# Normalising the heads' outputs inside the transposing product, and other pieces for the last token tile

## The chip, the cores and the metric

One Trainium2 chip, one core. The metric is the device time of one launch in microseconds; of several runs the median is given. A profile is one execution recorded by the hardware; its times are counted from the first instruction.

## What is computed

One layer of a hybrid backbone for 512 latent tokens and 128 context tokens (640 rows), width 1024, float32. From the reference, cut to what the change touches:

```
z = h @ w_in                                     # q, k, v, g_ret, x_lru, g_lru, m_ret, m_lru
o = o_f + o_b                                    # retention, 4 heads, 512 columns per head
o = o * rsqrt(mean(o * o, -1) + EPS)             # per token and head
o = o.reshape(B, L, D_RET_V) * gn_w * silu(g_ret)
ret_out = o @ w_ret_down
merged = sigmoid(m_ret) * ret_out + sigmoid(m_lru) * lru_out
out = x + gate * (merged @ w_out)
y = rmsnorm(out, final_norm_w)                   # y_sample (512 tokens), y_prompt (128 tokens)
```

The two recurrent (RG-LRU) directions and the cached states are computed beside it.

## The kernel before

Tokens are handled as five tiles of 128 (four of the latents, one of the prompt) or, transposed, as 640 columns. Products are made of split operands: a matrix is kept as a rounded part (float32r) and a rest, and `mm3` (L413) issues three products for one. Stage A makes most columns of z in transposed form and stores them to DRAM. Then come four heads; then the product with `w_ret_down` (the loop over `DOWN`, 128 output columns at a time, each in two halves of k), the product with `w_lru_down`, and `w_out` with the end.

For head h: `v_product` (four steps of 7.5 us of TensorE work each), `inter`, `scores`, `kv_state`, `attend`. `attend` adds up `o[t]` for the five token tiles (128 tokens by 512 columns, tokens on the partitions), with the squares' sums in `ssq`. The job `norm` (L1477) takes the root and the reciprocal into `rst` and multiplies each `o[t]` by its column on VectorE (L1486). Later, `y_unit(h, i)` (L1518) for i = 0 to 3 transposes the 128-column block i of the five `o[t]` into two PSUM banks `z` and `zp_` (L1522), with `ident` as the moving operand; a job multiplies that by the gate tile `sg` (L1532 for 512 columns, L1535 for 128) and stores it to DRAM, from where `y_job` loads it again as `yf` and splits it into `yh` and `yl` for the `DOWN` loop. The four units of heads 0 to 2 stand inside the next head's `v_product`; those of head 3 stand ahead of steps 1 and 2 of the `DOWN` loop, two and two. So there are 16 units of 5 transposes.

Order: TensorE's instructions come in the order of the code. ACT's and VectorE's come from a planner (`Plan`, L93), which keeps planned clocks for the engines, gives every operation a planned cost (`Vh(n)` is 0.55 n + 150 ns on VectorE, a unit is 560 ns on TensorE) and picks among the jobs that are ready by priority. Each engine then executes its own list in order. All DMAs are issued by SP, in the order in which they were written out.

Tiles: wide tiles (128x640) come from `W6`, with 11 places in the heads' stage. q and k of a head, split, take 8 of them from their loading until `scores` is over; gate tiles `sg` take one each until stored. `sg0` and `sg1` are loaded after `attend`, `sg2` after unit 0's job and `sg3` after unit 1's. A place given back with a store outstanding is planned as free 4 us later; the load that takes it waits for the store. Weights arrive in 512 KB pieces in 4 raw buffers and are split into 3 slab pairs. There are 8 PSUM banks.

The end: `w_out` is used token tile by token tile. Each tile is made in pieces of output columns (L1848): two of 512 for tiles 0 to 3; for tile 4, the prompt's, 512, 256 and 256. A piece is 24 products (8 k, three each), and then `finish_part` (L1790): product with the gate (L1800), add of the input (L1802), on ACT the squares' sum (L1804), product with the norm weight (L1806); a small sum (`finish_sum`, L1816 and L1818 in tile 4); and after the last piece `finish_end` (L1820): root on ACT, reciprocal (L1826), ACT scales the second 512 columns (L1832), VectorE the first (L1835), and SP issues a store of each (L1836), the second half's first. A job of a piece follows the job of the piece before it.

Of the kernel before, what the change touches and what calls it, by code (L numbers as in the profile page):

```python
# [12 lines left out]
MUL, ADD, SUB = ALU.mult, ALU.add, ALU.subtract  # L13
# [79 lines left out]
class Plan:  # L93
# [14 lines left out]
    def job(self, gen, name=None, prio=2.0):  # L108
        self.seq += 1
        j = Job(gen, prio, self.seq, self.time() + self.LAG)  # L110
        self.jobs.append(j)
        if name:
            self.named[name] = j
        self.advance(j)
        return j
# [64 lines left out]
    def need(self, name):  # L180
        j = self.named.get(name)
        assert j is not None, f"nothing makes {name}"
        self.finish(j, name)
# [77 lines left out]
def A(n, table=None):  # L261
    return ("act", 0.85 * n + 190.0, table)


def V(n):
    return ("dve", 1.042 * n + 150.0)


def Vh(n):
    return ("dve", 0.55 * n + 150.0)  # L270


def If(f):
    return ("if", f)
# [28 lines left out]
def tile_hybrid_step(  # L303
# [14 lines left out]
    nc = tc.nc  # L318
    S = Plan()
    act, dve, pool, pe = nc.scalar, nc.vector, nc.gpsimd, nc.tensor  # L320
# [13 lines left out]
    W6, WL = Slots(S), Slots(S)  # L334
# [5 lines left out]
    def wide(name, r=False):  # L340
        return W6.take([128, NT], F32R if r else F32, name)
# [45 lines left out]
    ident = cst.tile([128, 128], F32, name="ident")  # L387
# [15 lines left out]
    rst = cst.tile([128, 8], F32, name="rst")  # L403
# [9 lines left out]
    def mm3(out, lh, ll, rh, rl, start, stop, **kw):  # L413
        pe.matmul(out=out, lhsT=lh, rhs=rh, start=start, stop=False, **kw)  # L414
        pe.matmul(out=out, lhsT=lh, rhs=rl, start=False, stop=False, **kw)  # L415
        pe.matmul(out=out, lhsT=ll, rhs=rh, start=False, stop=stop, **kw)  # L416
        S.pe += 3 * (out.shape[-1] / 2.4 + 13.4)
# [4 lines left out]
    def bank():  # L422
        if not banks.items:
            S.until(lambda: banks.items)
        t = banks.take([128, 512], F32, "z")
        w = t_when.pop(id(t))
        if w > S.pe and S.cur is None:
            S.lost.append((S.pe, w - S.pe, "bank"))
            S.pe = w
        return t  # L430
# [167 lines left out]
    def store(key, t, w=NT):  # L598
        if key not in kept:
            kept[key] = scr.tile([128, w], F32, name="_".join(str(a) for a in key))  # L600
        nc.sync.dma_start(out=kept[key], in_=t[:, 0:w])
        stored[key] = arrives(128 * w * 4)
# [406 lines left out]
    def after(name):  # L1009
        return If(lambda: S.over(name))  # L1010
# [250 lines left out]
    def narrow(name, r=False):  # L1261
        return W5.take([128, 512], F32R if r else F32, name)
# [23 lines left out]
    def strip_job(h):  # L1286
        ds, s = d["ds"], d["strip"]
        yield Vh(896)
        dve.tensor_scalar(s, ds, sp[:, 24 + h:25 + h], None, op0=MUL)
        yield V(896)  # L1290
        dve.scalar_tensor_tensor(s, ds, lg[:, h:h + 1], s, op0=MUL, op1=ALU.min)
        yield A(896, "exp")
        act.activation(s, s, AF.Exp)

    qk, v, o, pt, kd = {}, {}, {}, {}, {}
# [166 lines left out]
    def attend(h):  # L1462
        def ev(t, ps):
            if t == 4:
                yield If(W5.room())
                o[t] = narrow("o")
                yield A(512)
                act.activation(o[t], ps, AF.Copy)
            else:
                yield after(f"i{h}{t}1")  # L1470
                yield V(512)
                dve.tensor_tensor(o[t], o[t], ps, op=ADD)
            yield A(512)
            act.activation(ps, o[t], AF.Square, accum_out=ssq[:, t:t + 1])
            banks.give(ps)

        def norm():  # L1477
            for t in range(5):
                yield after(f"o{h}{t}")
            yield A(5, "sqrt")  # L1480
            act.activation(rst[:, 0:5], ssq[:, 0:5], AF.Sqrt, scale=1.0 / DV, bias=epsc)
            yield V(5)
            dve.reciprocal(rst[:, 0:5], rst[:, 0:5])
            for t in range(5):
                yield Vh(512)
                dve.tensor_scalar(o[t], o[t], rst[:, t:t + 1], None, op0=MUL)  # L1486

        need(f"st{h}4")
        ps = bank()
        mm3(ps, pt[4][0], pt[4][1], v[4][0], v[4][1], True, True)  # L1490
        job(ev(4, ps), f"o{h}4", prio=1.0)
        for t in range(4):
            ps = bank()
            c = slice(128 * t, 128 * t + 128)
            for j in range(4):
                need(f"st{h}{j}")
                need(f"v{h}{j}")
                mm3(ps, pt[j][0][:, c], pt[j][1][:, c], v[j][0], v[j][1], j == 0, j == 3)
                S.pump()
            job(ev(t, ps), f"o{h}{t}", prio=1.0)  # L1500
        for i in range(5):
            for x in (pt[i] if i < 4 else ()) + v[i]:
                W5.give(x)
        job(norm(), f"y{h}", prio=1.0)
        job(strip_job(h + 1), f"strip{h + 1}", prio=3.0) if h + 1 < NH else None
        for i in range(4):
            job(sg_job(h, i), f"sg{h}{i}", prio=5.0)

    sg = {}

    def sg_job(h, i):
        if i > 1:
            yield after(f"yT{h}{i - 2}")
        yield If(is_kept(("g", h, i)))
        yield If(W6.room())
        sg[i] = fetch(("g", h, i), "sg")

    def y_unit(h, i):  # L1518
        need(f"y{h}")
        z, zp_ = bank(), bank()  # L1520
        for t in range(5):
            pe.transpose(z[:, 128 * t:128 * t + 128] if t < 4 else zp_[:, 0:128], o[t][:, 128 * i:128 * i + 128], ident)  # L1522
        S.pe += 560.0
        if i == 3:
            for t in range(5):
                W5.give(o.pop(t))

        def ev():
            yield after(f"sg{h}{i}")
            s = sg[i]  # L1530
            yield V(512)
            dve.tensor_tensor(s[:, 0:512], s[:, 0:512], z, op=MUL)  # L1532
            banks.give(z)
            yield V(128)
            dve.tensor_tensor(s[:, 512:640], s[:, 512:640], zp_[:, 0:128], op=MUL)  # L1535
            banks.give(zp_)
            store(("y", h, i), s)
            W6.give(s, 4000.0)

        job(ev(), f"yT{h}{i}", prio=1.2)  # L1540
        S.pump()
# [42 lines left out]
    for h in range(NH):  # L1584
        for kk in v_first if h == 0 else v_product(h):
            if h and kk:
                y_unit(h - 1, kk - 1)
            hook(h, f"v{kk}")
        if h:
            y_unit(h - 1, 3)  # L1590
        if h == NH - 1:
            hTp.__exit__(None, None, None)
            ytp, yr = open_pool("ytp", "right")
            yr.tile([128, 56], F32, name="edge")
            W6y.add(yr, [f"y{i}" for i in range(16)])
            for i in range(8):
                job(y_job(i // 4, i % 4, W6y), f"y_{i}", prio=3.0)
        inter(h)
        scores(h)
        if h + 1 < NH:  # L1600
            fetch_qk(h + 1)
        hook(h, "sc")
        kv_state(h)
        hook(h, "kv")
        attend(h)
        hook(h, "at")
# [116 lines left out]
    for m in range(8):  # L1723
        zs = [bank(), bank()]
        for k in range(NB):
            b = NB * m + k
# [29 lines left out]
        if m == 0:  # L1756
            b = bank()
# [62 lines left out]
    def finish_end(t, n):  # L1820
        q = fsq[:, 3 * t + n - 1:3 * t + n]
        pre = fsq[:, 15 + t:16 + t]
        yield A(1, "sqrt")
        act.activation(q, q, AF.Sqrt, scale=1.0 / D, bias=pre)
        yield Vh(1)
        dve.reciprocal(q, q)  # L1826
        dst = y_sample[128 * t:128 * t + 128, :] if t < 4 else y_prompt
        for b in (1, 0):
            u = fin_u[t, b][:, 0:512]
            if b:  # L1830
                yield A(512)
                act.activation(u, u, AF.Copy, scale=q)  # L1832
            else:
                yield Vh(512)
                dve.tensor_scalar(u, u, q, None, op0=MUL)  # L1835
            nc.sync.dma_start(out=dst[:, 512 * b:512 * b + 512], in_=u)  # L1836
            W6.give(fin_u[t, b], 4000.0)
            W6.give(xr[t, b])

# [6 lines left out]
    load_xr(0)  # L1846
    wo = {}
    parts = [(t, 512 * b, 512, b) for t in range(4) for b in range(2)]  # L1848
    parts += [(4, 0, 512, 0), (4, 512, 256, 1), (4, 768, 256, 2)]

    def finish(t, a, c0, n, i):
        end = 2 if t == 4 else 1
        if i:
            yield after(f"f{t}{i - 1}")
        yield from finish_part(t, a[:, 0:n], c0, n, i)
        banks.give(a)
        if i == end - 1:
            yield from finish_sum(t, end + 1)
        if i == end:
            yield from finish_end(t, end + 1)  # L1860
# [131 lines left out]
```

## Time and profile before

| | us |
|---|---|
| three runs, median (lowest to highest) | 999.16 (998.46 to 999.55) |
| profiled execution, its time | 999.01 |
| its span (first to last instruction) | 997.2 |
| TensorE matmul busy (PE) | 981.6 |
| TensorE weight load busy (PEld) | 918.0 |
| VectorE busy (DVE) | 732.3 |
| ScalarE busy (ACT) | 543.6 |
| GpSimd busy (POOL) | 2.2 |

PE and PEld are two views of TensorE: weight loads lie beside products, and products are pipelined, so the duration of one product (its latency) is longer than the distance from its start to the next one's. An idle time of an engine is listed with what ended it. The chain of work that ended last is followed back from the last instruction, at each step to what released it. The granted clock is TensorE's, as a share of 2.4 GHz; the profiled execution's mean is 0.997.

### The profile page before, as it was taken

Reading aid. Unit: us, or ns where it says so; the run is one execution under the profiler, and the core shown is the slowest. Engines: PE = TensorE matmul, PEld = TensorE weight load, DVE = VectorE, ACT = ScalarE, POOL = GpSimd, SP = SyncE. Lnnn points to the kernel's source line nnn. Section 1 sums busy time; section 2 is a strip of 40 time slices with the busy share of each in tenths; the row PEclk is TensorE's granted clock in tenths of the full one; section 3 lists DMA queues with packets and bytes.
Section 4 is the critical chain, followed back from the end, with each engine's and each line's share of the span. In section 5 each row is a group of like instructions: output and inputs, shape, how many; then the busy total and the mean of one; then the engine's idle time right before and its main releaser. Section 6 shows DMA issues by size and latency. Waiting matters only on the chain.

```text
span 997.2 us, 15542 instructions
## 1 busy us (share of the span) xinstructions
PE 981.6 (98%) x6079; PEld 918.0 (92%) x6079; DVE 732.3 (73%) x1133; ACT 543.6 (55%) x856; POOL 2.2 (0%) x13
## 2 busy tenths in 40 slices
PE   9999999999999999999999999999899999999997
PEld 8889999999999999999888888888789999999886
DVE  4699977779986799783775887877768877646554
ACT  6665554486544765652468596485574535324222
POOL 0000000000000000000000000000000000000000
PEclk9999999999999999999999999999999999999999
DMA  9745444333553335344532635454627554745312
GB/s 328 247 138 171 156 142 138 127 126 131 182 172 128 111 130 178 134 138 164 190 116 101 203 116 176 136 175 153 206 93 290 191 184 165 240 124 176 118 64 84
DMA packets 62167, 158.15 MB, mean 159 GB/s; under 512 B 6906, under 2 KB 10126, under 8 KB 62094
## 3 DMA queue, kind: packets, MB, share of 16 engines
q1 hardware_dynamic: 62094, 157.16, 46.9%
q8 instruction: 47, 0.77, 0.3%
q14 instruction: 26, 0.21, 0.1%
HBM read 119.51 MB, written 37.63 MB: 158 GB/s over the span
## 4 chain that ended last, share of the span: by engine, by line
PE 91%; DVE 4%; ACT 3%; issue 1%; DMA 1%; POOL 0%; DVEq 0%; POOLq 0%; ACTq 0%
PE z L414 29%; PE z L415 29%; PE z L416 29%; PE b L736 1%; PE z L1522 1%; ACT hf L294 1%; DVE sl L420 1%; ACT hTh L294 1%; DVE hTl L294 1%; DMA y<-sg 0%; DMA yf<-y 0%; ACT sh L539 0%; PE z L781 0%; ACT gt L1181 0%; DVE st L1416 0%
## 5 line engine op out<-in xcount | busy, mean ns | idle before, releaser
L420 DVE TENSOR_TENSOR sl<-raw,sh 128x1024 fp32r<-128x1024 f32 (+1 forms) x128 | 133.2, 1045 | 50.2 <-ACT sh L505 49.8
L505 ACT ACTIVATE sh<-raw 128x1024 fp32r<-128x1024 f32 (+1 forms) x96 | 96.8, 1013 | 120.2 <-PE z L415 75.9
L414 PE MATMUL z<-sh,sh 128*128 128x320 f32 x512 | 158.5, 310 | 0.7 <-ACT p L1007 0.7
L416 PE MATMUL z<-sh,sl 128*128 128x320 f32 x512 | 158.4, 309 | 0.0
L415 PE MATMUL z<-sl,sh 128*128 128x320 f32 x512 | 158.4, 309 | 0.0
L414 PE MATMUL z<-hTh,sh 128*128 128x320 f32 x432 | 134.6, 311 | 1.1 <-ACT hTh L294 1.1
L415 PE MATMUL z<-hTl,sh 128*128 128x320 f32 x432 | 133.4, 309 | 0.7 <-DVE hTl L294 0.7
L416 PE MATMUL z<-hTh,sl 128*128 128x320 f32 x432 | 133.2, 308 | 0.0
L414 PEld LDWEIGHTS z<-sh,sh 128*128 128x128 f32 x512 | 96.1, 188 | 1.3 <-ACT p L1007 1.3
L415 PEld LDWEIGHTS z<-sl,sh 128*128 128x128 f32 x512 | 96.1, 188 | 0.0
L416 PEld LDWEIGHTS z<-sh,sl 128*128 128x128 f32 x512 | 96.1, 188 | 0.0
L414 PEld LDWEIGHTS z<-hTh,sh 128*128 128x128 f32 x432 | 81.1, 188 | 3.9 <-issue 2.5
L415 PEld LDWEIGHTS z<-hTl,sh 128*128 128x128 f32 x432 | 81.1, 188 | 1.1 <-DVE hTl L294 1.1
L416 PEld LDWEIGHTS z<-hTh,sl 128*128 128x128 f32 x432 | 81.1, 188 | 0.0
L414 PE MATMUL z<-yh,sh 128*128 128x320 f32 x256 | 79.4, 310 | 1.6 <-ACT gt L1181 1.5
L415 PE MATMUL z<-yl,sh 128*128 128x320 f32 x256 | 79.2, 309 | 1.0 <-DVE yl L420 1.0
L416 PE MATMUL z<-yh,sl 128*128 128x320 f32 x256 | 79.0, 309 | 0.0
L414 PE MATMUL z<-sh,hTh 128*128 128x512 f32 x160 | 63.7, 398 | 0.0
L415 PE MATMUL z<-sl,hTh 128*128 128x512 f32 x160 | 63.2, 395 | 0.0
L416 PE MATMUL z<-sh,hTl 128*128 128x512 f32 x160 | 63.2, 395 | 0.0
L1054 ACT ACTIVATE p<-z 128x320 f32<-128x320 f32 x32 | 14.0, 437 | 67.3 <-PE z L416 67.3
L414 PEld LDWEIGHTS z<-yh,sh 128*128 128x128 f32 x256 | 48.1, 188 | 2.2 <-ACT gt L1181 1.7
(256 smaller groups left out, 2240.3 us busy)
## 6 DMA issues: line engine op xcount, KB each, us to landing
raw<-in_w_str_dram SPq DMA_DIRECT2D x131, 512.0 KB, 3.8
adr<-in_w_ada_dram SPq DMA_DIRECT2D x32, 256.0 KB, 5.9
g<-c SPq DMA_DIRECT2D x16, 320.0 KB, 2.1
sg<-g SPq DMA_DIRECT2D x16, 320.0 KB, 4.0
y<-sg SPq DMA_DIRECT2D x16, 320.0 KB, 2.2
yf<-y SPq DMA_DIRECT2D x16, 320.0 KB, 4.6
out_dram<-kv SPq DMA_DIRECT2D x16, 256.0 KB, 2.8
x<-c SPq DMA_DIRECT2D x10, 320.0 KB, 4.0
```

The costliest lines, as they stand in the source:

```text
L294: return f(*args, **kw)
L414: pe.matmul(out=out, lhsT=lh, rhs=rh, start=start, stop=False, **kw)
L415: pe.matmul(out=out, lhsT=lh, rhs=rl, start=False, stop=False, **kw)
L416: pe.matmul(out=out, lhsT=ll, rhs=rh, start=False, stop=stop, **kw)
L420: dve.tensor_tensor(out, full, f32(hi), op=SUB)
L505: act.activation(hi[:, 0:w], raw, AF.Copy)
L736: pe.matmul(out=mb[1][:, 384:512], lhsT=ident, rhs=ident, start=True, stop=True)
L1054: act.activation(self.tmp[:, 2], self.a[:, 0:H], AF.Copy)
L1522: pe.transpose(z[:, 128 * t:128 * t + 128] if t < 4 else zp_[:, 0:128], o[t][:, 128 * i:128 * i + 128], ident)
```

## The change

Four edits. `norm` no longer multiplies `o[t]`; it takes a wide tile `dy` and writes into it five 128x128 diagonals, the identity with each row times that token's `rst`. `y_unit` makes `o[t]` block transposed, times the diagonal, as an ordinary float32 product, in place of the transpose with `ident`; the planned 560 ns of a unit are unchanged. `dy` is given back after the fourth unit. The last token tile's pieces are 512, 384 and 128 columns, and the store of its second half is issued from ACT's queue, the first half's from SP's.

```diff
@@ norm (in attend)
             dve.reciprocal(rst[:, 0:5], rst[:, 0:5])
+            yield If(W6.room())
+            dy[0] = wide("dy")
             for t in range(5):
-                yield Vh(512)
-                dve.tensor_scalar(o[t], o[t], rst[:, t:t + 1], None, op0=MUL)
+                yield Vh(128)
+                dve.tensor_scalar(dy[0][:, 128 * t:128 * t + 128], ident, rst[:, t:t + 1], None, op0=MUL)
@@
-    sg = {}
+    sg, dy = {}, {}
@@ y_unit
         for t in range(5):
-            pe.transpose(z[:, 128 * t:128 * t + 128] if t < 4 else zp_[:, 0:128], o[t][:, 128 * i:128 * i + 128], ident)
+            pe.matmul(out=z[:, 128 * t:128 * t + 128] if t < 4 else zp_[:, 0:128], lhsT=o[t][:, 128 * i:128 * i + 128],
+                      rhs=dy[0][:, 128 * t:128 * t + 128], start=True, stop=True)
         S.pe += 560.0
         if i == 3:
             for t in range(5):
                 W5.give(o.pop(t))
+            W6.give(dy.pop(0))
@@ finish_end
-            nc.sync.dma_start(out=dst[:, 512 * b:512 * b + 512], in_=u)
+            (nc.scalar if t == 4 and b else nc.sync).dma_start(out=dst[:, 512 * b:512 * b + 512], in_=u)
@@
-    parts += [(4, 0, 512, 0), (4, 512, 256, 1), (4, 768, 256, 2)]
+    parts += [(4, 0, 512, 0), (4, 512, 384, 1), (4, 896, 128, 2)]
```

## Rows read from the trace of the kernel before

**Rows 1.** The page, part 1: busy time, share of the span, instructions.
```profile
PE 981.6 (98%) x6079; PEld 918.0 (92%) x6079; DVE 732.3 (73%) x1133; ACT 543.6 (55%) x856; POOL 2.2 (0%) x13
```
**Rows 2.** The page, part 4: the chain that ended last, by engine.
```profile
PE 91%; DVE 4%; ACT 3%; issue 1%; DMA 1%; POOL 0%; DVEq 0%; POOLq 0%; ACTq 0%
```
**Rows 3.** Waits of PE: us in total, times, longest.
```profile
PE z L414 <- ACT pph L1419: 2.9, 1, 2.9
PE z L414 <- ACT gt L1181: 1.5, 1, 1.5
...
PE z L415 <- DVE yl L420: 1.0, 1, 1.0
```
**Rows 4.** Groups by line and shape, PE: count, busy us, mean ns, idle.
```profile
L736 PE MATMUL b<-ident 128*128 128x128 f32 x114 | 15.2, 299 | 1.4 <-POOL ident masks.py:199 1.4
...
L1522 PE MATMUL z<-ident,o 128*128 128x128 f32 x80 | 10.7, 272 | 0.0
...
L1433 PE MATMUL z<-q,k 128*128 128x128 f32 x16 | 2.4, 273 | 0.0
```
**Rows 5.** The chain, in order of time: start, us, what.
```profile
547.58 0.55 PE z L1522 x5
...
583.92 0.45 PE z L1433 x4
```
**Rows 6.** Waits of PEld, of the bank after the last units.
```profile
PEld z L414 <- DVE sg L1532: 0.4, 1, 0.4
```
**Rows 7.** L1486 on DVE (ns min/median/max, first, last); first unit in PE's timeline.
```profile
L1486 DVE TENSOR_SCALAR o<-o,rst x20: 476/480/488, 538.3 to 739.1; 128x512 f32<-128x512 f32 x20
...
547.42 0.71 PE L1522 MATMUL z<-ident,o 128*128 128x128 f32 x5
```
**Rows 8.** SP: issues in the timeline after unit 0; waits, 690 to 720.
```profile
548.97 0.32 SPq L601 DMA_DIRECT2D y<-sg  x1
549.34 0.42 SPq L606 DMA_DIRECT2D sg<-g  x1
...
SPq L606 <- DMA y<-sg: 7.5, 3, 4.0
```
**Rows 9.** PE's timeline, last tile: start us, us, instruction.
```profile
984.88 0.39 PE L416 MATMUL z<-sh,ml 128*128 128x512 f32 x1
985.11 0.28 PE L414 MATMUL z<-woh,mh 128*128 128x256 f32 x1
...
987.96 0.28 PE L414 MATMUL z<-woh,mh 128*128 128x256 f32 x1
```
**Rows 10.** DVE's timeline, last tile.
```profile
985.31 0.69 DVE L1800 TENSOR_TENSOR u<-z,ga 128x512 f32<-128x512 f32 x1 [2.33 <-PE z L416]
...
988.16 0.42 DVE L1800 TENSOR_TENSOR u<-z,ga 128x256 f32<-128x256 f32 x1 [0.70 <-PE z L416]
...
989.81 0.15 DVE L1818 TENSOR_SCALAR fsq<-fsq 128x1 f32<-128x1 f32 x1
990.99 0.42 DVE L1800 TENSOR_TENSOR u<-z,ga 128x256 f32<-128x256 f32 x1 [1.03 <-PE z L416]
```
**Rows 11.** ACT's timeline, last tile.
```profile
986.76 0.60 ACT L1804 ACTIVATE z<-xr 128x512 f32<-128x512 f32 x1 [3.48 <-DVE xr L1802]
...
989.08 0.39 ACT L1804 ACTIVATE z<-xr 128x256 f32<-128x256 f32 x1 [1.59 <-DVE xr L1802]
...
993.04 0.72 ACT L1832 ACTIVATE u<-u,fsq 128x512 f32<-128x512 f32 x1 [0.29 <-DVE fsq L1826]
```
**Rows 12.** Stores of the result on SP: ns min/median/max, first and last start.
```profile
L1836 SPq DMA_DIRECT2D out_dram<-u x10: 332/364/384, 954.4 to 994.2; - x10
```
**Rows 13.** After PE's longest wait: chain; busy time with granted clock, 722 to 724.
```profile
722.34 0.42 PE z L414
...
725.32 0.40 PE z L415
...
722.00:724.00 2.00, 2.00 (x7) 1.59 (x6) 1.90 (x6) 1.97 (x6) 0.00 (x0) 0.54 0.35 130
```

## The prediction, written before the result

> **What bounds the kernel now.** I read the engine shares on the first page first, then the chain that ended last, then the waits of TensorE, then stretches of the timeline. TensorE is busy for 981.6 of 997.2 us and VectorE for 732.3 [rows 1]; the chain of the work that ended last lies on PE for 91% of the span and on DVE for 4% [rows 2]. Of PE's waits after the start three matter: 2.9 us for the score tile `pph`, 1.5 us for an eviction of a gate product, 1.0 us for a split y tile [rows 3]. So an instruction added to PE is paid nearly in full, and VectorE's work is worth something only where PE stands behind it. The end is different: after the last product PE is idle, and a short chain on DVE and ACT and two stores set the time.
>
> The profiled execution took 999.01 us, the span and 1.8 us around it, and the median of the runs is 999.16; the sum below is made against 999.0.
>
> **Part 1, the diagonal: PE.** Each `y_unit` had 5 transposes, 16 units make 80. In the rows by shape these are 80 matrix records (L1522) [rows 4]. The reader is to see next that an ordinary f32 product leaves two records: the 8 products of `scores` for the prompt (4 heads, k = 0, 1) appear as 16 at L1433, and the 57 of the warming loops (8, 5 times 9, twice 2) as 114 at L736 [rows 4]. The new product is of that kind: f32, stationary `o`, moving 128 columns of the diagonal. The 272 ns of a record is its latency and not its share of the stream, so I take the pitch from the chain: 5 transposes took 0.55 us, that is 0.11 each; 2 f32 products of the same 128x128 shape (4 records) took 0.45 us, that is 0.22 each [rows 5]. A unit goes from 0.55 to 5 x 0.225 = 1.12 us, +0.57, and 16 of them are +9.0 us (8.8 if the record is 0.110). PE has no gap there, so nothing hides it. Bounds: 0, if the new product streams like a transpose, and three more transposes' time each, 80 x 0.33 = 26.4 us, if it takes four records' time; I take 9.0, because the row of the same shape says so.
>
> What is given back: the last pair of units (head 3, i = 2 and 3) is followed by two accumulators for which no bank is free; PE waits 0.4 us for VectorE's product `sg` [rows 6]. With the units 0.57 us longer VectorE, which starts on a unit's 512 columns when its fourth product is done, has released the banks before PE asks: -0.4. The other waits are not shortened, since their chains begin with PE's own work and move with it.
>
> The Trainium skill ("TensorE: Matmul & The Clock Gate", Terms) calls the transposing mode four times faster for FP32. Rows 5 show twice (0.11 against 0.22). By the skill part 1 would be +26.4 us; I keep the row.
>
> **Part 1, VectorE.** 20 operations of 128x512 at 480 ns, five per head [rows 7], become 20 of 128x128. No such tensor_scalar is in the trace; one column costs 0.15 us (L1818) [rows 10] and 512 cost 0.48, so between 0.15 and 0.48, near 0.23 on the line through both: 20 x 0.25 = 5 us less work, between 0 and 6.6. It is worth nothing: the first head's five start at 538.3, end by 540.7, and its first transpose begins at 547.4 [rows 7], so over 6 us of v products hide the normalisation already. Its cover cannot go, as it gets shorter.
>
> **Part 1, the slot.** `dy` takes one of the 11 wide tiles of the heads' stage, from the normalisation until the fourth unit. 8 hold q and k of the next head, so 3 are free, and two are taken by `sg0` and `sg1`. In the trace `sg2` takes the third: its load is issued 0.37 us after the store of y0, without a wait [rows 8]. After the change it must have `sg0`'s tile, and so wait for that store to land; SP, which issues in order, stands meanwhile, with the next weight load behind it. A wait of this kind is in the trace: `yf` loads waited 7.5 us for y stores in three times, 4.0 the longest [rows 8]. `sg2` and `sg3` are needed some 14 us after the unit that frees their tile, and weights are loaded into 4 buffers ahead of 3 slabs, so I cost it at 0; if the cover failed, one such wait, +4.0, would reach PE.
>
> The order of ACT's and DVE's work comes from planned costs, and the normalisation is planned some 1 us shorter, while the units are still planned at 560 ns. That can reorder jobs; I can't derive it and keep it in the range.
>
> **Part 2, the last token tile.** It has three pieces. Before: the second (256 columns) starts on PE at 985.11; the third (256) starts 24 products later at 987.96, so 0.119 us each; the last 512-column product steps by 0.23 [rows 9]. The line through both gives 0.174 for 384 columns: 24 x 0.174 = 4.17 instead of 2.85. For 128 columns of the split (fp32r) kind the trace has no row, all are 256 and wider. From below the same line gives 0.063; the nearest rows in width are the 128-column f32 ones: 0.11 a record, 0.22 a whole product [rows 5]. I take 0.22, as the narrow f32 product is the only one of that width that isn't a transpose, and keep the rest for the range.
>
> VectorE began on the third piece at 990.99, 5.88 us after the second's first product; it had been done with the second since 989.96 and waited for PE [rows 9, 10]. After, with 0.22: 4.17 + 24 x 0.22 + 0.18 = 9.63 us, so 3.75 later. The chain behind it gets shorter: a 128x512 product on VectorE is 0.69 and a 128x256 one 0.42, so 128 columns are near 0.28, twice 0.14 less; ACT's square goes from 0.39 towards 0.29 (0.60 at 512) [rows 10, 11]: -0.38 in all. Stores: SP issues the second half's store when ACT is done (993.04 + 0.72 = 993.76), and the first half's after it, at 994.2, although VectorE had that half ready sooner [rows 11, 12]. With ACT issuing its own, both are out at about 993.8: -0.4. An issue on ACT's queue isn't in the trace; I take SP's 0.36 [rows 12], and bound the gain by 0 and 0.4. Net: +3.75 - 0.38 - 0.40 = +3.0.
>
> **Sum:** 999.0 + 9.0 - 0.4 + 3.0 = 1010.6 us.
>
> **Rivals.** (a) Narrow products are cheap. With 0.063 the end is set by VectorE: it starts on the second piece 4.37 us after its first product, and its chain there, with 384 columns, is 2.22 long (the trace's 1.80 from 988.16 to the end of L1818 and three operations of 0.14 more) [rows 10], so the third begins at 6.6 instead of 5.88: +0.73 - 0.78, about 0; at 0.11 a product it is PE again: 6.99, +0.3. The time is 1007.6 to 1007.9. For it: at 256 columns and up the cost falls with the width; against it, that nothing narrower is shown. The skill's same page (Back-to-back issue gap) gives about 81 ns for N=128 in a stream of loads and products; no run here shows it, and its 131 ns for N=512 is not what rows 9 show (0.23). By it the sum would be 1007.6.
>
> (b) The slot decides: loads of gate tiles wait for stores on SP, and weights come late once: +4.0, 1014.6 (1011.7 with cheap narrow products). For it: every `sg2` and `sg3` of three heads gets the wait. Against it: the buffers ahead.
>
> (c) The reordered plan removes the stall before head 3's attention: 2.9 us of waiting, and behind it 8 products of 512 columns step by 0.42 instead of 0.23, in a stretch where the granted clock is 0.54 of full, near the lower of its two levels (1.2 GHz) [rows 3, 13]: -1.6. That is -4.5, 1006.1. The stall comes from a `yf` load that waits for a store's tile, and which tile is free there is what `dy` changes. It may also grow.
>
> (d) The product costs four transposes' time, 0.44: 26.4 instead of 9.0 for part 1, +17.4 on the forecast, 1028. Rows 5 speak against it. It is what the skill's rule above would make of it.
>
> (e) The other side, not slower: the diagonal's product streams at the transposes' 0.11 us, since the array takes the same 128 columns. Then part 1 is 0 (and the bank wait stays), and with cheap narrow products the end is even: 999.0. It decides if a unit stays at 0.55 us. The two records per product of L1433 and L736 speak against it. That the change doesn't normalise inside the product can't be: it is written there.
>
> **Chances.** Forecast 0.46 (its own range 1009.6 to 1011.6); (a) 0.30; (b) 0.08; (c) 0.08; (d) 0.03; (e) 0.05. From 1005.8 to 1013.4 lie the forecast, (a), and about half of (b) and (c): 0.84. About 0.2%, 2 us, is what a measurement of this kernel can tell from no change: slower 0.95, as all but (e) are; within 0.03; faster 0.02, when (e) meets (c).
>
> **What would show it.** L1522 with 160 matrix records in place of 80, and 10 of them in 1.12 us per unit on the chain: right; 0.55 or 2.2 us: wrong. The time from the last piece's first to its last product: 5.3 us for 24 (forecast), 1.5 to 2.6 (a). VectorE waiting for PE before its last 128 columns (forecast), or PE done first (a). The last two stores issued within 0.4 us of each other from two queues. PE's waits at `pph` still about 3 us; a new wait of PE for weights (`sh` or `sl`) would be (b). L1486 near 0.25 us each, and nobody waiting for it.

## The result, and the profile after

| | before | after |
|---|---|---|
| six runs each, median (lowest to highest), us | 999.22 (998.46 to 999.55) | 1008.62 (1006.90 to 1011.41) |
| ratio, with its 95% interval | | 1.0097 [1.0081, 1.0114] |
| profiled execution, us (span; granted clock) | 999.01 (997.2; 0.997) | 1009.84 (1008.0; 0.996) |

The change makes the kernel 9.4 us slower by the medians; 1010.6 was forecast. The profiled executions are 10.8 us apart, more than the medians, since the runs of after fall into groups by their mean granted clock: at 0.999 three runs took 1006.9 to 1007.7, at 0.996 two took 1009.5 and 1009.8, at 0.992 one took 1011.4. The profiled one is of the middle group. This matters below.

**Where the time went.** The first two parts of the page, engine by engine and then the chain that ended last, answer to [rows 1, 2]:

```profile
PE 992.3 (98%) x6159; PEld 929.5 (92%) x6159; DVE 728.9 (72%) x1133; ACT 543.9 (54%) x856; POOL 2.2 (0%) x13
...
PE 90%; DVE 4%; ACT 3%; DMA 2%; issue 1%; SPq 0%; POOL 0%; DVEq 0%; POOLq 0%; ACTq 0%
```

TensorE is busy for 10.7 us more, with 80 matrix records more, and that is nearly the whole difference; VectorE is busy for 3.4 us less and nothing came of it. By line, the new product and the new diagonal (ns minimum, median, maximum, then the first and last start) answer to [rows 4, 7], and the chain of waits (start, us, what) to [rows 5]:

```profile
L1524 PE MATMUL z<-dy,o x160: 270/275/275, 548.3 to 765.9; 128*128 128x128 f32 x160
...
L1488 DVE TENSOR_SCALAR dy<-ident,rst x20: 278/280/289, 539.2 to 746.5; 128x128 f32<-128x128 f32 x20
```

```profile
695.28 1.11 PE z L1524 x10
```

Five products leave ten records and take 1.11 us, where five transposes took 0.55. I laid the starts of all other products side by side in the two traces. Each unit moves what follows it by 0.56 to 0.57 us more, and the last two of the 16, in head 3, move it by 0.77 together instead of 1.14: the 0.4 us for the bank [rows 6] is gone. Net +8.7.

PE's waits, in the order of their length, answer to [rows 3], and the granted clock (the seventh column, ahead of the DMA share) behind the longest of them to [rows 13]:

```profile
PE z L414 <- ACT pph L1419: 3.5, 1, 3.5
PE z L414 <- ACT gt L1181: 1.5, 1, 1.5
...
PE z L415 <- DVE yl L420: 0.9, 1, 0.9
```

```profile
731.00:733.00 2.00, 2.00 (x6) 1.54 (x5) 1.93 (x5) 2.00 (x5) 0.00 (x0) 0.50 0.19 72
```

The stall ahead of head 3's attention grew from 2.9 to 3.5 us, and behind it TensorE ran at half clock as before. One execution each is little to judge this place by: experiment 1 below has the code of after up to there and shows 3.9, experiments 2 and 5 have that of before and show 3.0 and 2.5.

The last token tile, PE first, then VectorE and ACT with its queue (start, us, instruction, in brackets the idle time before it), answers to [rows 9 to 12]:

```profile
995.23 0.34 PE L414 MATMUL z<-woh,mh 128*128 128x384 f32 x1
...
999.43 0.22 PE L414 MATMUL z<-woh,mh 128*128 128x128 f32 x1
...
999.59 0.28 PE L416 MATMUL z<-woh,ml 128*128 128x128 f32 x1
...
1001.94 0.27 PE L416 MATMUL z<-sh,ml 128*128 128x128 f32 x1
```

```profile
1002.25 0.29 DVE L1804 TENSOR_TENSOR u<-z,ga 128x128 f32<-128x128 f32 x1 [0.44 <-PE z L416]
```

```profile
1003.92 0.72 ACT L1836 ACTIVATE u<-u,fsq 128x512 f32<-128x512 f32 x1 [0.29 <-DVE fsq L1830]
1004.68 0.38 ACTq L1840 DMA_DIRECT2D out_dram<-u  x1
```

384 columns step by (999.43 - 995.23) / 24 = 0.175 us. 128 columns step by (1001.94 - 999.59) / 21 = 0.112 us, half of the 0.22 that I took. VectorE begins on the last piece 7.02 us after the second's first product (5.88 before) and still waits for PE, 0.44 us. From the second piece's first product to the end of ACT's last operation it is 9.41 us (1003.92 + 0.72 - 995.23), where it was 8.65 (993.04 + 0.72 - 985.11): +0.76. From there to the end of the span it is 3.36 instead of 3.44: -0.08.

So the 10.8 us of the profiled pair are +8.7 for the units, +0.6 for the stall, +0.7 for the tail, and 0.8 to 0.9 in small steps: among the warming products at the start, whose step falls from 0.21 to 0.11 us at 5.4 us before and at 6.6 us after (0.6), and spread thinly over all products (0.3). The last two are differences of one execution from another.

### The profile page after: what moved, and what is told of

It is laid out like the page before. It is cut to its first block, busy times and chain, and to the rows that moved or that the text cites. A ratio compares the mean times of both kernels' runs of the same rounds, so it can differ in the third digit from the quotient of the medians.

```text
span 1008.0 us, 15705 instructions
## 1 busy us (share of the span) xinstructions
PE 992.3 (98%) x6159; PEld 929.5 (92%) x6159; DVE 728.9 (72%) x1133; ACT 543.9 (54%) x856; POOL 2.2 (0%) x13
## 4 chain that ended last, share of the span: by engine, by line
PE 90%; DVE 4%; ACT 3%; DMA 2%; issue 1%; SPq 0%; POOL 0%; DVEq 0%; POOLq 0%; ACTq 0%
PE z L414 29%; PE z L415 29%; PE z L416 29%; PE z L1524 2%; PE b L736 2%; DMA y<-sg 1%; DMA yf<-y 1%; ACT hf L294 1%; DVE sl L420 1%; ACT hTh L294 1%; DVE hTl L294 1%; ACT sh L539 0%; PE z L781 0%; DVE st L1416 0%; DVE s L846 0%
```

## The experiments

All were timed in five rounds beside the kernel before on the same chip. That kernel's median was 999.17 in the first group, 998.43 in the second, 999.39 in the third and 999.59 beside the last run, so ratios are compared.

**1. The first part alone**

```diff
-            (nc.scalar if t == 4 and b else nc.sync).dma_start(...)
+            nc.sync.dma_start(...)
...
-    parts += [(4, 0, 512, 0), (4, 512, 384, 1), (4, 896, 128, 2)]
+    parts += [(4, 0, 512, 0), (4, 512, 256, 1), (4, 768, 256, 2)]
```

> The diagonal alone: pieces of the last tile 512, 256, 256 and all stores on SP, as before. Theory: the last tile's new pieces and queues cost +0.7 us, all the rest is the diagonal, so this one takes about 1007.9 us (0.7 under the changed kernel), with 160 matrix records in the units and 0.57 us more per unit. Rival (the new end saves time, as shorter pieces and two queues should): it is slower than the changed kernel, about 1009.3 us.

Measured: 1008.22 us (1006.10 to 1010.73), ratio 1.0090 [1.0075, 1.0104]. The diagonal carries nearly all of the loss.

**2. The second part alone**: the same lines the other way round, in the kernel before.

> The last tile's pieces 512, 384, 128 and the two store queues alone, transposes as before. Theory: a product of 128 columns costs 0.112 us against 0.119 at 256, so the third piece saves almost nothing while the second costs 24 x 0.055 = 1.3 us more; 0.4 comes back in VectorE's and ACT's chain and 0.1 in the stores: +0.7, 999.9 us. The record's forecast (0.22 per narrow product) would give 1002.2; the rival that the end gets shorter gives 998.8 or less.

Measured: 999.99 (999.60 to 1001.39), ratio 1.0011 [1.0002, 1.0020]. The tail costs about 1 us; +3.0 lies outside the interval, and a gain too. In the trace it is less: from the second piece's first product to the end of the span it is 12.6 us (985.4 to 998.0), 12.1 in the kernel before (985.1 to 997.2): +0.5.

**3. The kind of product alone**: the identity in place of the diagonal, the normalisation left where it was.

```diff
-            pe.transpose(z[:, ...], o[t][:, 128 * i:128 * i + 128], ident)
+            pe.matmul(out=z[:, ...], lhsT=o[t][:, 128 * i:128 * i + 128], rhs=ident, start=True, stop=True)
```

> The kernel before with each unit's transposes made as ordinary f32 products with the identity: normalisation on VectorE as before, no diagonal, no slot taken. Theory: the whole price of the diagonal is the kind of product, 80 x 0.113 = 9.1 less 0.4 of a bank wait that goes: 1007.9 us, 160 records. Rival (the slot and the changed order of jobs carry part of it): 1005 us or less here.

Measured: 1008.31 (1005.48 to 1009.79), ratio 1.0096 [1.0081, 1.0111]. This kernel has VectorE's old 20 operations of 512 columns and no diagonal, and loses as much as experiment 1. What costs is that an f32 product takes the place of a transpose. That VectorE has less to do shows no gain, within the 2 us or so that the two intervals leave; in the trace of before no engine waits for L1486.

**4. The diagonal's tile alone**: taken, written and held until the fourth unit, read by nobody; transposes and normalisation as before.

```diff
+            yield If(W6.room())
+            dy[0] = wide("dy")
+            for t in range(5):
+                yield Vh(128)
+                dve.tensor_scalar(dy[0][:, 128 * t:128 * t + 128], ident, rst[:, t:t + 1], None, op0=MUL)
...
+            W6.give(dy.pop(0))
```

> The kernel before, normalisation and transposes as before, but the diagonals are made beside it and their wide tile is held until the fourth unit; nothing reads them. Theory: PE's units are untouched, SP waits for gate tiles' stores are there, and only PE's wait for pph may grow by 0.6: 999.2 to 999.8 us. Rival (the slot decides): 1001 us or more, with new waits of PE.

Measured: 996.02 (995.67 to 996.52), ratio 0.9968 [0.9957, 0.9980]. It is faster, which neither theory had. PE's wait at `pph`, and the stretch behind it with its clock:

```profile
PE z L414 <- ACT pph L1419: 1.9, 1, 1.9
```

```profile
719.60:721.60 2.00, 2.00 (x9) 1.63 (x10) 1.97 (x4) 1.69 (x3) 0.00 (x0) 1.00 0.46 175
```

The wait is 1.0 us shorter and the clock does not fall after it, which saves 8 products some 0.2 us each, 1.6 in all [rows 13]; the span is 2.6 us shorter than before's. So the stall is worth more than its own length, and the order of small things ahead of it seems to decide it. The next experiments ask what makes it.

**5. What a narrow product costs**: the kernel before with 512, 320 and 192 columns.

```diff
-    parts += [(4, 0, 512, 0), (4, 512, 256, 1), (4, 768, 256, 2)]
+    parts += [(4, 0, 512, 0), (4, 512, 320, 1), (4, 832, 192, 2)]
```

> The kernel before with the last token tile in parts of 512, 320 and 192, one store queue. What a narrow split product costs is open: 128 columns took 0.112 us in the changed kernel, 256 took 0.119. Theory floor (below about 256 columns a product does not get cheaper): 320 columns 0.147 each on the line between 0.119 and 0.23, 192 columns 0.112 to 0.116; TensorE's part 24 x 0.147 + 24 x 0.114 + 0.18 = 6.45 us instead of 5.88, the chain behind it 0.19 shorter, time +0.4 = 999.5. Theory double rate (below 256 columns each column costs twice, so 128 columns land at 0.112 by chance): 192 columns take 0.168, TensorE's part 7.74 us, time +1.7 = 1000.9. Theory line (cost falls on with the width): 0.091.

Measured: 999.57 (998.04 to 1001.76), ratio 1.0007 [0.9998, 1.0015]. PE's timeline:

```profile
985.57 0.31 PE L414 MATMUL z<-woh,mh 128*128 128x320 f32 x1
...
989.10 0.25 PE L414 MATMUL z<-woh,mh 128*128 128x192 f32 x1
...
989.30 0.27 PE L416 MATMUL z<-woh,ml 128*128 128x192 f32 x1
...
991.31 0.27 PE L416 MATMUL z<-sh,ml 128*128 128x192 f32 x1
```

The last two lines are 18 products apart: 0.112 us each. 128 columns take 0.112, 192 take 0.112, 256 take 0.119 [rows 9]: it is a floor, and neither the line nor a price per column. 320 columns take (989.10 - 985.57) / 24 = 0.147. The time is 0.7 us above before's, 0.4 was expected; the interval holds both.

**6. A longer planned time until a gated tile is free**: the plan alone; no operation is added or removed.

```diff
-            W6.give(s, 4000.0)
+            W6.give(s, 9000.0)
```

> The kernel before, only that the plan counts a gated tile as free 9 us after its store is issued instead of 4 us. Theory S (the stall at pph comes from a yf load placed on the tile of a y store that is still under way, with VectorE's split of that yf in the middle of the attention's operations): the yf goes elsewhere or later, the wait at pph falls from 2.9 to under 1.9 us, the granted clock does not fall behind it, and the time is 994.7 to 996.5. Rival (VectorE has just that much work there): wait 2.9, time 999.2 within 0.5.

Measured: 994.88 (994.51 to 997.17), ratio 0.9967 [0.9955, 0.9979]. In the kernel before, the chain into the stall is a load of `yf` that gets the tile of a y store still under way, and behind it the split that VectorE has in its order ahead of the attention's operations:

```profile
704.54 3.68 DMA y<-sg
708.23 3.35 DMA yf<-y
711.60 0.75 ACT yh L1553
712.38 0.83 DVE yl L420
713.20 0.66 DVE o L1365
...
720.65 0.50 PE z L414
```

With 9 us the y store is no longer on it, and the split that VectorE does there comes earlier:

```profile
711.04 0.83 DVE yl L420
711.88 3.91 DMA yf<-y
715.81 0.74 ACT yh L1553
716.55 0.53 ACT pth L1419
...
719.94 0.50 PE z L414
```

```profile
PE z L414 <- ACT pph L1419: 1.1, 1, 1.1
```

The wait is 1.8 us shorter, the clock stays, and the 1.5 us for `gt` are gone as well. Experiments 10 and 11 have the same code up to here and wait 1.4 and 2.0 us in their profiled executions, and behind the 2.0 the clock falls: the plan makes this wait shorter, it doesn't fix it.

**7. The y loads given to the plan later**

```diff
-            for i in range(8):
-                job(y_job(i // 4, i % 4, W6y), f"y_{i}", prio=3.0)
         inter(h)
         scores(h)
+        if h == NH - 1:
+            for i in range(8):
+                job(y_job(i // 4, i % 4, W6y), f"y_{i}", prio=3.0)
```

> The kernel before with the eight y split jobs given to the plan after the last head's score products instead of ahead of them. Theory S: no yf is in VectorE's order ahead of the operations that pph needs, the wait at pph goes (under 1 us) with the half clock behind it, time 994.7 to 996; if the splits then come late for the down projections, a wait for yl appears and gives part of it back (up to 998). Rival: the wait stays at 2.9 because VectorE's other work sets it, 999.2.

Measured: 995.94 (995.57 to 996.65), ratio 0.9973 [0.9963, 0.9984]. The wait at `pph` is gone altogether, while waits for `gt` (1.0) and for `yl` (two, 1.5 together) stay. Two different edits of the same load's place give nearly the same time, which supports the chain above.

**8. A wide tile more, a narrow one less**

```diff
-        W5.add(hd, [f"n{i}" for i in range(25)])
-        W6.add(hd, [f"w{i}" for i in range(11)])
+        W5.add(hd, [f"n{i}" for i in range(24)])
+        W6.add(hd, [f"w{i}" for i in range(12)])
```

> The kernel before with 12 wide and 24 narrow tiles in the heads' stage instead of 11 and 25. Theory S: with a tile more the yf loads need not take the tile of a store under way; the wait at pph is under 1.9 us and the time 994.7 to 996.5, unless the missing narrow tile makes a wait of its own (then up to 1000). Rival (tiles don't matter): wait 2.9, 999.2.

Measured: 1011.03 (1009.66 to 1013.31), ratio 1.0126 [1.0110, 1.0142]; the longest wait is now another one:

```profile
PE z L414 <- ACT pth L1419: 13.1, 1, 13.1
```

This wait is in head 1's attention (593 to 606 us). At `pph` PE waits 0.5 us, which is what the theory had, but both numbers of tiles changed, and the order with them, so this doesn't show what the wide tile does. The theory's case for it is left open. What it shows is how steep the plan is here: one tile exchanged for another made a wait of 13 us.

**9. The whole change with 9 us**

> The whole change with the plan's 9 us instead of 4 us for a gated tile. Theory S holds in the changed kernel too: the stall at pph (3.5 us there) and the clock behind it go, and what is left of the change against the kernel before with the same 9 us (994.9) is the products' 16 x 0.565 - 0.38 = +8.7 and the tail's +0.7: 1004.3 (1003.4 to 1005.2). Rival (the changed kernel's stall has a cause of its own, the load of sg that waits for a tile now, with SP standing meanwhile): wait 3 us or more, 1008 to 1009.

Measured: 1008.33 (1007.15 to 1009.72), ratio 1.0094 [1.0081, 1.0108]. The theory missed by 4 us; the rival has the time, but not its wait of 3 us or more. The wait at `pph` is still 2.2, the one for `gt` still 1.5, and SP's waits (690 to 735) show two kinds ahead of the loads at L606:

```profile
SPq L606 <- DMA y<-sg: 10.2, 4, 3.4
...
SPq L606 <- PE z L1524: 5.1, 1, 5.1
```

The second is a load of `yf` that waits for the last product that reads the diagonal's tile, with all that SP has behind it. Both kinds are in the changed kernel with 4 us too (11.9 and 5.0).

**10. The store queue with 9 us**, parts of 512, 256 and 256 kept; the diff is experiment 6's line and `nc.scalar` for the last two stores.

> The kernel before with 9 us, three parts of 512, 256, 256 as before, and the last token tile's second and third store from ACT's queue. Read from the changed kernel's trace (ACT's packets begin 1.19 us after the issue, SP's 0.83): -0.1, 994.8. By the prediction's term: -0.4, 994.5. Rival (a second queue costs at the program's end): +0.3, 995.2.

Measured: 995.03 (994.49 to 995.93), ratio 0.9959 [0.9947, 0.9972], the same as experiment 6's within their intervals. The last store is issued at 990.0 on ACT's queue and the span ends at 993.2; in experiment 6 it is issued at 990.2 on SP's, and the span ends at 993.2. But the last tile begins later here. The second piece's first product, in experiment 6 and in this one:

```profile
981.07 0.28 PE L414 MATMUL z<-woh,mh 128*128 128x256 f32 x1
...
981.32 0.28 PE L414 MATMUL z<-woh,mh 128*128 128x256 f32 x1
```

From there to the end it is 12.1 us in experiment 6 and 11.9 here, so the second queue gains about 0.25 us, which is too little for these times to show.

**11. The whole tail with 9 us**

> The kernel before with 9 us and the whole second part of the change (512, 384, 128 and two queues), so without the stall whose clock varies from run to run. Theory: +0.7 over 994.9, 995.6. The prediction's forecast of this part: +3.0, 997.9. Rival (even): 994.9.

Measured: 995.60 (994.99 to 997.74), ratio 0.9969 [0.9957, 0.9980]: +0.6 over experiment 10 by the medians, which differs from it in the parts alone. The intervals overlap; the traces, not the times, carry the size of this term. From the second piece's first product (983.26) to the end of the span (995.9) it is 12.6 us, as in experiments 2 and 9: +0.75 for the parts, -0.25 for the queue, +0.5 together.

**12. The product against the identity with 9 us**: experiments 3 and 6 together, no diagonal.

> The product against the identity in place of the transposes, normalisation and tail as before, no diagonal's tile, and the plan's 9 us. The whole change with 9 us took 1008.3 (wait at pph 2.2, gate wait 1.5), the kernel before with 9 us 994.9 (1.1, none): 13.4 us apart, of which the products' 8.7 and the tail's 0.7 are known. Theory slot (the rest is the diagonal's tile: loads of sg wait for stores, SP stands, the yf loads come late): without the tile the rest goes, 994.9 + 8.7 = 1003.6 (1002.6 to 1004.8), wait at pph 1.5 or less. Rival (the units' length alone moves the operations against each other and brings the stall back): 1006.5 to 1008, wait at pph 2 us or more.

Measured: 1004.88 (1003.29 to 1006.72), ratio 1.0055 [1.0041, 1.0068]. PE's wait is nearly that of experiment 6:

```profile
PE z L414 <- ACT pph L1419: 1.2, 1, 1.2
```

Against experiment 6 it is 1.0055 - 0.9967 = 0.0088 of 999, 8.8 us, which is the units' 8.7 (8.6 in the two traces, product by product); by its median it lies 0.1 above the theory's range. Against experiment 9 it is 3.9 us faster, 0.5 to 0.7 of which is the tail; about 3 us (with an uncertainty of some 2) are the diagonal under that plan, its tile and the order of operations that comes with it, which no run holds apart. Laid side by side, the two traces part at three places: 0.9 us at `pph`, 1.6 at `gt` and 1.0 among the products with y at 770 us. Under the plan as it was, experiments 1 and 3 are equal within their intervals (some 2 us), so no cost of the tile shows there; with the transposes, in experiment 4, it gained 3.

**A faster version.** Experiments 4, 6, 7, 10 and 11 are 3 to 4 us faster than the kernel before. The simplest is the kernel before with 9000 instead of 4000 in one line: 994.88, ratio 0.9967 [0.9955, 0.9979].

## Why the prediction was right or wrong

The direction and its cause were right: one term, +9.0 for 80 f32 products, is the loss. Experiment 3 isolates it, and experiment 12 gives it as 8.8 with the stall out of the way. It came from two rows, the 2 records per f32 product and the 0.45 us for two such products on the chain [rows 4, 5]. A unit takes 1.11 us, neither the 2.2 of rival (d) nor the 0.55 of rival (e), and both fall with it. The Trainium skill ("TensorE: Matmul & The Clock Gate", Terms) calls the transposing mode four times faster for FP32; at this width it is twice (1.11 against 0.55 us).

The bank wait's -0.4 is seen in the trace, and VectorE's saving shows no worth, as said (experiment 3 has none of it and takes as long, within some 2 us). The diagonal's tensor_scalar took 0.28 us, between the bounds of 0.15 and 0.48 and above the 0.25 that I took; nobody waits for it.

**The step that failed is "I take 0.22"**: the narrow split product costs 0.112. The nearest row in width was of another kind of product, and I took its whole price and not that of one record, 0.11, which was the right figure. With 0.112 my own formula gives 24 x 0.174 + 24 x 0.112 + 0.18 = 7.04 us, and 7.02 was measured: the frame was right and the price wrong. The chain behind it came out as forecast, 0.38 shorter (from VectorE's start on the last piece to the end of ACT's last operation 2.39 us instead of 2.77). The tail came to +0.7 in the profiled pair, and to +0.5 in experiments 2, 9 and 11, instead of +3.0. On this rival (a) was right, though its bottom, even, was not: at 0.112 VectorE still waits for PE. The Trainium skill's figure for a narrow product in a stream of loads and products ("TensorE: Matmul & The Clock Gate", Back-to-back issue gap, about 81 ns) is lower than the 0.112 of this trace.

The stores' -0.4 was -0.1 in the profiled pair and about -0.25 elsewhere. The last issue does come 0.4 us sooner, 0.04 behind ACT's operation (1004.68 against 1004.64) where it was 0.44, but the span ends 3.3 us after it (1004.7 to 1008.0) instead of 3.0 (994.2 to 997.2). In experiments 2, 9, 10 and 11, which use ACT's queue too, it ends 3.2 us after it, in experiment 6, on SP's, 3.0. So the profiled execution of after ended 0.1 to 0.2 us later than the queue explains.

The stall at `pph` was a rival (c), with "it may also grow" behind it. It grew by 0.6 in the profiled pair. What I did not see is how much this place moves by itself: the six runs of after spread over 4.5 us, and the longer a run took, the lower is its mean granted clock. The profiled pair therefore differs by more than the medians. Experiment 7 shows (c)'s price to be right: its trace, laid beside that of before, gains 4.6 us from the wait to the end of the slow products (4.5 forecast), 1.5 of which later waits take back. Experiments 4 and 6 keep a part of the wait and gain some 3 us in all. Only it did not happen in this change.

Rival (b), the slot: the waits of SP that I foresaw are there. Between 540 and 731 SP waits 18.9 us for y stores in 8 places (7.5 in 3 before), and the load of `sg2` is issued 2.1 us after the store of y0 instead of 0.4 [rows 8]:

```profile
SPq L606 <- DMA y<-sg: 18.9, 8, 5.5
...
550.31 0.32 SPq L601 DMA_DIRECT2D y<-sg  x1
552.44 0.32 SPq L606 DMA_DIRECT2D sg<-g  x1
```

What of it reaches PE depends on the plan: nothing that the times show with the plan as it was, about 3 us with the plan of experiment 9, not as a wait for weights but at `pph`, at `gt` and in the loop over `DOWN`. So "costed at 0" held for this kernel within some 2 us, but the tile has no price of its own: it was -3, 0 and +3 in three surroundings.

With the tail at +0.5 to +0.7 the sum would have been 1008.1 to 1008.3, and the median is 1008.6. The narrow product's price was 2.6 us too high (24 x 0.108), while the stores gained 0.15 to 0.3 less than forecast, and 1010.6 was 2.0 too high. The few tenths that are left are less than the stall moves from run to run.

## What to carry to other kernels

Fold a scale into a transposing product only where TensorE has slack: an f32 product of 128 columns left two matrix records and took 0.22 us here where a transpose left one and took 0.11, and the work saved on another engine counts only if TensorE waits for it. Price an instruction from the row of its own kind, and when only a shape is missing, look for the floor (here about 0.11 us a matrix record, split or f32) before a line is drawn through wider shapes. Where a planner places loads, look at which store each load's tile waits for; one planned time moved this kernel by over 3 us with not an operation added.

## What the runs showed of the hardware that was not expected

- Split (fp32r) products step by 0.112 us at 128 and at 192 columns, 0.119 at 256, 0.147 at 320, 0.175 at 384 and 0.23 at 512, each with a weight load of its own; f32 transposes step by 0.11 and f32 products leave two records of 0.11. Whether the weight load sets the floor was not tried.
- A wait of 2.9 us on TensorE is followed by eight products of 512 columns that step by 0.43 us instead of 0.23, at a granted clock of 0.50 of full (the lower level, 1.2 GHz): with 1.6 us for these it costs 4.5. After waits of 1.1, 1.9 and 2.2 us (experiments 6, 4 and 9) the profiled executions show 1.00; those of experiments 11 and 5 wait 2.0 and 2.5 and their clock falls. So the length of the wait alone does not decide it.
- The clock also falls where no edit comes near. In the stretch from 56 to 62 us the profiled executions of experiments 1, 5, 10 and 11 show 0.77, 0.72, 0.74 and 0.74, all others 1.00. The same stretch in experiments 6 and 10 (the granted clock is the seventh column, ahead of the DMA share):

```profile
56.00:62.00 6.00, 6.00 (x43) 6.00 (x43) 5.96 (x9) 5.34 (x7) 0.00 (x0) 1.00 0.35 111
...
56.00:62.00 6.00, 6.00 (x33) 6.00 (x32) 5.93 (x10) 5.10 (x7) 0.00 (x0) 0.74 0.57 193
```

- In the six runs of after the time follows the mean granted clock (0.999, 0.996, 0.992: some 2 us a step). In experiment 9 it doesn't (1008.33 at 0.999, 1007.15 at 0.998), so the clock is not all that varies there; what else does was not found.
- A last store on ACT's queue ends the program later after its issue than one on SP's: 3.2 us in experiments 2, 9, 10 and 11 (3.3 in after), against 3.0 in seven of the nine kernels that use SP's alone (3.1 in experiment 8, 3.5 in experiment 1). That takes 0.15 to 0.2 of the 0.4 that the earlier issue gives.
